# A one-core decoder block whose instruction order is planned: a stored order table, one wide constant table, other early buffers and loads

## The chip, the core and the metric

The kernel runs on one core of one Trainium2 chip. The metric is the device time of one execution in microseconds (us); the kernel before takes 552.94 us (median of three runs, 551.5 to 555.01). Five engines work side by side, each through its own instructions in their given order: TensorE (PE: matmuls, and the weight loads ahead of them, PEld), VectorE (DVE), ScalarE (ACT), GpSimd (POOL) and SyncE (SP), which here issues all DMAs. Engines wait for each other and for DMAs by semaphores.

## The reference

One decoder block on 256 tokens of width 1024, all in float32. Cut to what matters:

```python
h = rmsnorm(x, g_pre_mix)
z = h @ w_in                                  # 8248 columns, split into the branches' inputs
o_cmp, p_cmp = nsa_compressed(q, k0, v0, ...) # blocks of 32 tokens through a small MLP (w1, silu, w2)
o_slc = nsa_selected(q, k2, v2, ...)          # with 256 tokens all causal blocks are chosen
o_win = nsa_window(q, k4, v5)
y_nsa = gb[0] * o_cmp + gb[1] * o_slc + gb[2] * o_win
y_ml  = sigmoid(o_ml) * headnorm(mlstm(conv_silu(q, k), v, i, f)) * ml_head_g
kv    = rmsnorm(mem, g_mem) @ w_mem_kv        # the memory's keys (512 columns) and values (512)
y_mem = softmax(q_mem @ k.T * scale) @ v
y = gm[0] * (y_nsa @ w_proj_nsa) + gm[1] * (y_ml @ w_proj_ml) + gm[2] * (y_mem @ w_proj_mem)
x = x + rmsnorm(y @ w_out, g_post_mix)
h = rmsnorm(x, g_pre_ffn)
gate, up = split(h @ w_ffn_in)                # 2 x 2816 columns
x = x + rmsnorm((silu(gate) * up) @ w_ffn_down, g_post_ffn)
```

## The kernel before

**Products in three parts.** Every float32 operand of a product is split in two: `hi` is its copy rounded to the matmul's short float32 (ACT writes it: `whi` of a weight, `hh` of the normed x, `mh` of the memory), `lo` is what is left (DVE subtracts: `wlo`, `hl`, `ml`). A product is hi*hi + hi*lo + lo*hi, three matmuls into one PSUM tile (`mm3`). PSUM tiles of the dense products are called `pd` and `pss`; which of the two pools a tile takes says nothing of its content.

**Weights in units.** All weights stream from one array `W` in units of 128 x 1024 float32 (512 KB), one DMA each into a tile `raw` (four buffers), then `whi` (ACT) and `wlo` (DVE), four buffers each. `tmaj` multiplies tokens by four such units with the weights as the moving side (matmuls of 512 columns), `fpair` and `fcat` have the weights as the stationary side. The units' names are the matrices': `mem_k` 0 to 3, `mem_v` 0 to 3, `kv` 0 to 11 and so on.

**The stages.** (1) The memory: `memt` (the memory, transposed) is scaled to `mh`/`ml` by `mem_in`, which needs the gains in `vc` (from `vec`). The first three units of `mem_k` and their slices of `memt` come in halves, so that work can start early. The keys are 96 matmuls into two `pd` tiles, the values 48 matmuls of 512 columns into two `pss` tiles. The memory's sum of squares goes over `msq` (ACT squares, DVE adds), `col` (PE, two small matmuls by a column of ones), `rv` (DVE), `rm` (POOL, power -0.5) to `rbc` (PE, copies the row to all partitions). (2) The norm of x the same way: `sq`, `col`, `rv`, `rr`, `rbc`; then `xt` is scaled and split to `hh`/`hl`, eight slices of each. (3) `kv` 0 to 3, whose results go to `st` (ACT and DVE) and through `ph`, the small MLP of the compressed blocks, with weights `w1`. (4) Gates, memory attention, the three NSA attentions (four groups, two halves of 128 tokens each) with the mLSTM and the merge gates filled in between. (5) The three projections and the merge (`mrg`, `yh`/`yl`). (6) `w_out`: four `tmaj` products; `scaled` takes each result's sum of squares (`sq`, `ss`), its product with the gains (`zg`, `z`), and for 128 tokens at a time (`tb` 0 and 1) adds x into `xg`, transposes it (`ptx1`: four PE transposes for each half of the columns) and splits it to `xc` (hi and lo), the input of the FFN. (7) The FFN: `ffn_gate` and `ffn_up` for the first 512 columns, then 36 units by `fcat`, then `ffn_down`. Four units of the first `ffn_gate` product are kept in tiles `wq`.

**What sets the order.** `block_kernel` does not issue instructions as it is written. `Plan.record` notes each as an `Op` with its dependencies; `Plan.schedule` then lists them: at each step the engine that is free first takes, of its ops that are ready by a table of costs, the one of the lowest rank. A rank is the op's place in the code, moved by `plan.later(n)` (n places later) and by `boost` (a number for each op, which brings it forward). A tag's buffers are handed out in that order too. `Plan.replay` goes through an order with the same costs and finds what each PE op lost by waiting. `choose` tries 12 pairs of two cost settings (`matmul`, `slack`), takes the best by `replay`, and makes 40 rounds of random boosts along the chains that PE waited for, keeping those that `replay` finds no longer. `issue` emits the order that is left. All instructions are therefore issued in one line of the source (L511), and the rows of the profile are told apart by tile names.

**Where the change touches it.** `cs` (the constant table `cst` up to `K_M0`, with the identity `ident` in its first 128 columns), `rw` (the head gains and gate biases, a row that a DMA copies to all partitions), `w2t` (the compressed blocks' second weights), `mraw` (the masks), the DMAs ahead of the first norm, the tags of the two `w1` tiles (`G`, three buffers, of which `memt`, `mh` and `ml` are the first users), the three gain rows `g1`, `gp`, `go`, and the loop that transposes after `w_out`.

## Time and profile before

| | |
|---|---|
| three runs | 552.94, 551.5, 555.01 us |
| the profiled execution | 552.94 us, its span 551.1 us (first to last instruction) |
| PE busy | 539.2 us of the span (98%), 3164 matmul records |
| DVE, ACT, POOL busy | 422.5 (77%), 342.7 (62%), 20.5 us (4%) |
| DMA | 95.45 MB, mean 173 GB/s |
| granted TensorE clock, mean | 0.994 |

A matmul's row begins when its columns start to stream and ends, by a model, when the last result is out; rows of neighbours overlap. The step from one start to the next is what a matmul costs PE. A fp32 matmul that is not split in hi and lo (`ph`, `warm`) stands as two records. The profiled execution's own time is the median itself, so 552.94 us is what changes are counted from; 1.8 us of it lie around the span.

### The profile page before, as it was taken

How to read it: one execution, taken by the hardware profiler on the slowest of the kernel's cores; microseconds unless marked ns; L12 is line 12 of the kernel's file. 1: busy time of each engine (PE TensorE's matmuls, PEld its weight loads, DVE VectorE, ACT ScalarE, POOL GpSimd, SP SyncE). 2: the span in 40 equal slices, each digit the busy share in tenths (PEclk: the TensorE clock that was granted, in tenths of full speed). 3: DMA queues.
4: the chain of work that ended last, by engine and by line, in shares of the span. 5: the costliest groups of instructions: out<-in, count | busy, mean ns of one | idle time of the engine just before them, and what ended most of it. 6: DMA issues, size and time to landing. Idle time of an engine off the chain costs nothing.

```text
span 551.1 us, 8728 instructions
## 1 busy us (share of the span) xinstructions
PE 539.2 (98%) x3164; PEld 472.0 (86%) x3164; DVE 422.5 (77%) x813; ACT 342.7 (62%) x672; POOL 20.5 (4%) x34
## 2 busy tenths in 40 slices
PE   8899999999999999999999999999999999999995
PEld 8789999998989889889888888778888888888884
DVE  4797697589899897996888687975778787854543
ACT  6755777574699776875896444764666666643430
POOL 0010000000000100100100000000000000000000
PEclk9899999999999999999999999999999999999998
DMA  7966336734633354255254656753555555565512
GB/s 264 312 261 230 118 113 185 233 120 132 213 111 118 119 189 152 80 170 210 88 182 160 217 196 196 235 180 121 175 189 184 191 185 186 189 192 191 191 72 76
DMA packets 29419, 95.45 MB, mean 173 GB/s; under 512 B 3392, under 2 KB 6720, under 8 KB 29120
## 3 DMA queue, kind: packets, MB, share of 16 engines
q1 hardware_dynamic: 29376, 94.89, 52.0%
q8 instruction: 25, 0.41, 0.3%
q14 instruction: 18, 0.15, 0.1%
HBM read 92.78 MB, written 1.05 MB: 170 GB/s over the span
## 4 chain that ended last, share of the span: by engine, by line
PE 92%; DVE 3%; DMA 2%; issue 1%; ACT 1%; SPq 0%; DVEq 0%; ACTq 0%
PE pd L511 49%; PE pss L511 29%; PE sc L511 3%; PE pvn L511 2%; PE ptn L511 2%; PE ph L511 2%; DMA memt<-in_memT 1%; DMA raw<-in_W 1%; DVE wlo L511 1%; PE pn L511 1%; DVE wq L511 1%; PE psm L511 1%; DVE z L511 1%; PE pvm L511 1%; PE pq L511 1%
## 5 line engine op out<-in xcount | busy, mean ns | idle before, releaser
L511 DVE TENSOR_TENSOR wlo<-raw,whi 128x1024 fp32r<-128x1024 f32 (+1 forms) x161 | 193.6, 1206 | 66.7 <-ACT whi L511 63.3
L511 ACT ACTIVATE whi<-raw 128x1024 fp32r<-128x1024 f32 (+1 forms) x161 | 167.6, 1044 | 101.6 <-PE pd L511 57.0
L511 PE MATMUL pd<-hh,whi 128*128 128x256 f32 x224 | 64.3, 287 | 0.0
L511 PE MATMUL pd<-hh,wlo 128*128 128x256 f32 x224 | 64.1, 286 | 0.0
L511 PE MATMUL pd<-hl,whi 128*128 128x256 f32 x224 | 63.7, 285 | 0.2 <-DVE hl L511 0.2
L511 PE MATMUL pd<-whi,hh 128*128 128x512 f32 x144 | 58.8, 409 | 0.0
L511 PE MATMUL pd<-wlo,hh 128*128 128x512 f32 x144 | 58.3, 405 | 0.0
L511 PE MATMUL pd<-whi,hl 128*128 128x512 f32 x144 | 56.8, 397 | 0.0
L511 PEld LDWEIGHTS pd<-hl,whi 128*128 128x128 f32 x224 | 42.8, 191 | 0.6 <-DVE hl L511 0.4
L511 PE MATMUL pss<-xc,whi 128*128 128x512 f32 x168 | 43.2, 392 | 0.0
L511 PEld LDWEIGHTS pd<-hh,whi 128*128 128x128 f32 x224 | 42.8, 191 | 0.4 <-ACT hh L511 0.2
L511 PEld LDWEIGHTS pd<-hh,wlo 128*128 128x128 f32 x224 | 42.8, 191 | 0.2
L511 PE MATMUL pss<-whi,u 128*128 128x512 f32 x132 | 42.4, 392 | 0.0
L511 PEld LDWEIGHTS pss<-xc,whi 128*128 128x128 f32 x168 | 30.7, 189 | 5.4
L511 PE MATMUL pd<-xc,whi 128*128 128x512 f32 x120 | 31.9, 394 | 0.0
L511 PEld LDWEIGHTS pd<-whi,hl 128*128 128x128 f32 x144 | 27.1, 188 | 4.8
L511 PEld LDWEIGHTS pd<-whi,hh 128*128 128x128 f32 x144 | 27.2, 189 | 4.3
L511 PEld LDWEIGHTS pd<-wlo,hh 128*128 128x128 f32 x144 | 27.3, 189 | 3.9
L511 PEld LDWEIGHTS pss<-whi,u 128*128 128x128 f32 x132 | 24.8, 188 | 5.5
L511 ACT ACTIVATE pp<-sc,mx 128x128 f32<-128x128 f32 (+1 forms) x64 | 26.9, 433 | 1.4 <-DVE mx L511 1.4
L511 PE MATMUL pss<-wlo,u 128*128 128x512 f32 x66 | 25.9, 392 | 0.0
L511 DVE TENSOR_REDUCE mx<-sc 128x1 f32<-128x16 f32 (+2 forms) x96 | 22.3, 288 | 4.0 <-PE sc L511 3.8
(324 smaller groups left out, 1115.4 us busy)
## 6 DMA issues: line engine op xcount, KB each, us to landing
raw<-in_W SPq DMA_DIRECT2D x159, 512.0 KB, 4.2
w<-in_w SPq DMA_DIRECT2D x2, 1024.0 KB, 6.6
raw<-in_W SPq DMA_DIRECT2D x6, 256.0 KB, 4.0
xt<-in_xT SPq DMA_DIRECT2D x2, 512.0 KB, 8.5
kk<-kk SPq DMA_DIRECT2D x8, 128.0 KB, 4.7
x<-in_xN SPq DMA_DIRECT2D x2, 512.0 KB, 3.8
out<-z SPq DMA_DIRECT2D x8, 128.0 KB, 2.0
memt<-in_memT SPq DMA_DIRECT2D x6, 128.0 KB, 3.9
```

Of the source, the lines that this page charges most:

```text
L511: op.ins_ = getattr(op.real, op.method)(*map(arg, op.a), **{k: arg(x) for k, x in op.kw.items()})
```

## The change

It puts these things in place of the ones before:

- the order's table: `MATMUL, SLACK = 8.0, 30.0` and `BOOST`, a stored number for each of 241 ops; `choose` lists the ops once with these, and tries nothing. Two costs of the table are others (a DMA's cost and its landing time).
- the constant table `cst` is 720 columns wider: `rw` and `w2t` are slices of `cs` now, loaded with the masks' neighbours by one DMA, and their own two DMAs are gone. The three gain rows are stored 128 times in DRAM and read as plain tiles.
- in the code's order x comes ahead of `mem_v`, and `mem_v` 2 and 3, `kv` 0 to 3 and `w1` come ahead of the norms; `w1` lies in the tags `C` and `V`, one buffer each, whose next users are the convolution's `cy` and the values `vs`.
- the transposes after `w_out` have another rank: for `tb` 0 they stand 100 places earlier, for `tb` 1 as written.

The diff, cut:

```diff
+BOOST = {
+    0: 4320, 2: 90, 14: 580, 15: 560, 18: 4410, 19: 850, 20: 340, 96: 270, 97: 830, 122: 20, 127: 40, 128: 110, 129:
...
+}
+MATMUL, SLACK = 8.0, 30.0
-K_ID, K_TRI, K_RV, K_BM, K_M0, K_C1, K_MT, K_END = 0, 128, 256, 257, 261, 533, 549, 677
+K_ID, K_TRI, K_RV, K_BM, K_RW, K_W2, K_M0 = 0, 128, 256, 257, 261, 781, 973
+K_C1, K_MT, K_END = K_M0 + 272, K_M0 + 288, K_M0 + 416
...
-            return math.prod(views[0].shape) * 4 / 330.0
+            return math.prod(views[0].shape) * 4 / 410.0 + 70
...
-    START, TABLE, ISSUE, LAND = 570.0, 1283.0, 460.0, 1700.0
+    START, TABLE, ISSUE, LAND = 570.0, 1283.0, 460.0, 2000.0
...
-        best = None
-        for matmul in self.MATMUL:
-            for slack in self.SLACK:
...
-        return self.schedule(matmul, slack, boost)
+        order = self.schedule(MATMUL, SLACK, BOOST)
+        self.chosen = self.replay(order), MATMUL, SLACK, BOOST
+        return order
...
-    rw = one.tile([P, 520], F32, name="rw")
+    rw = cs[:, K_RW:K_RW + 520]
+    w2t = cs[:, K_W2:K_W2 + 192]
-    w2t = one.tile([P, 192], F32, name="w2t")
...
+    for h in range(2):
+        dma(out=xt[:, 4 * h:4 * h + 4, :], in_=xT[:, 4 * h:4 * h + 4, :])
     fetch(("mem_v", 0))
     fetch(("mem_v", 1))
-    for h in range(2):
-        dma(out=xt[:, 4 * h:4 * h + 4, :], in_=xT[:, 4 * h:4 * h + 4, :])
     dma(out=cs[:, 0:P], in_=cst[:, 0:P])
+    for u in (2, 3):
+        fetch(("mem_v", u))
+    fetch(("kv", 0))
+    fetch(("kv", 1))
+    w1t = []
+    for j, tg in enumerate("CV"):
+        t = bigt(tg, 1, [P, 16, P], F32, f"w1_{j}")
+        w1t.append(t)
+        dma(out=t, in_=w1[j].rearrange("p (a n) -> p a n", a=16))
+    fetch(("kv", 2))
+    fetch(("kv", 3))
...
-    fetch(("kv", 0))
-    fetch(("kv", 1))
     dma(out=wgt, in_=wg)
     dma(out=cs[:, P:], in_=cst[:, P:K_M0])
     mraw = work.tile([P, K_END - K_M0], F32, tag="sq", bufs=3, name="mraw")
     dma(out=mraw, in_=cst[:, K_M0:])
-    dma(out=rw, in_=bass.AP(tensor=row.tensor, offset=row.offset, ap=[[0, P], [1, 520]]))
-    dma(out=w2t, in_=w2)
...
-    w1t = []
-    for j in range(2):
-        t = bigt("G", 3, [P, 16, P], F32, f"w1_{j}")
-        w1t.append(t)
-        dma(out=t, in_=w1[j].rearrange("p (a n) -> p a n", a=16))
...
-    for t, i in ((g1, 520), (gp[:, 0, :], 520 + 2 * D), (go, 520 + D)):
-        dma(out=t, in_=bass.AP(tensor=row.tensor, offset=row.offset + i, ap=[[0, P], [1, D]]))
+    for i, t in enumerate((g1, gp[:, 0, :], go)):
+        dma(out=t, in_=row[i])
...
-        for q in range(2):
+        with plan.later(tb * 100 - 100):
+            for q in range(2):
...
-    row = np.concatenate([a[n] for n in ("ml_head_g", "ml_gate_b", "g_post_mix", "g_post_ffn", "g_pre_ffn")], axis=1)
+    row = np.stack([np.broadcast_to(a[n], (P, D)) for n in ("g_post_mix", "g_pre_ffn", "g_post_ffn")])
...
+    cst[:, K_RW:K_RW + 512] = a["ml_head_g"]
+    cst[:, K_RW + 512:K_RW + 520] = a["ml_gate_b"]
+    cst[:, K_W2:K_M0] = np.concatenate([w2k, w2k, a["cmp_w2_v"][0]], axis=1)
```

What the order becomes, at three places. The numbers behind the names tell tiles apart; they differ between the two programs. All rows stand in L511 before and in L505 after.

**SP, the queue of DMAs, from the tenth row on.** Before: `raw_137` is `mem_k` 2, `raw_204` is `mem_k` 3, `raw_222`, `raw_237`, `raw_263` and `raw_285` are `mem_v`, `xt` is x, `memt` 128x512 is the memory's last quarter.

```order
L511 DMA raw_137<-in_W 128x512
L511 DMA memt_97<-in_memT 128x256
L511 DMA raw_137<-in_W 128x512
L511 DMA xt_169<-in_xT 128x1024
L511 DMA memt_97<-in_memT 128x512
L511 DMA raw_204<-in_W 128x1024
L511 DMA raw_222<-in_W 128x1024
L511 DMA raw_237<-in_W 128x1024
L511 DMA xt_169<-in_xT 128x1024
L511 DMA cs_257<-in_cst 128x128
L511 DMA raw_263<-in_W 128x1024
L511 DMA raw_285<-in_W 128x1024
```

After: `raw_155` is `mem_k` 2, `raw_168` is `mem_k` 3, `raw_241` to `raw_308` are `mem_v`.

```order
L505 DMA raw_155<-in_W 128x512
L505 DMA raw_168<-in_W 128x1024
L505 DMA memt_74<-in_memT 128x256
L505 DMA raw_155<-in_W 128x512
L505 DMA memt_74<-in_memT 128x512
L505 DMA xt_214<-in_xT 128x1024 x2
L505 DMA raw_241<-in_W 128x1024
L505 DMA raw_268<-in_W 128x1024
L505 DMA cs_284<-in_cst 128x128
L505 DMA raw_291<-in_W 128x1024
L505 DMA raw_308<-in_W 128x1024
```

`mem_k` 3 has moved ahead of the last `memt` slices, and both halves of x stand between these and `mem_v`. In the rows ahead of these, `vc` has moved from fourth to third, and the first row is a slice of `memt` where it was a half unit of weights.

**DVE and PE, from the last keys to the first values.** On DVE before, `wlo_243` is the lo part of `mem_k` 3, `wlo_254` and `wlo_277` of `mem_v` 0 and 1, `msq` is the memory's sum of squares, `sq` that of x:

```order
L511 SCALAR_TENSOR_TENSOR ml_119<-memt_97,vc_102,mh_116 128x256 x2
L511 TENSOR_TENSOR msq_162<-msq_162,msq_234 128x1024
L511 TENSOR_TENSOR wlo_243<-raw_204,whi_239 128x1024
L511 TENSOR_TENSOR msq_162<-msq_162 128x512
L511 TENSOR_TENSOR wlo_254<-raw_222,whi_249 128x1024
L511 TENSOR_TENSOR msq_162<-msq_162 128x256
L511 TENSOR_TENSOR wlo_277<-raw_237,whi_265 128x1024
```

After, where `wlo_195` is the second half of `mem_k` 2 and `wlo_297` is `mem_v` 0:

```order
L505 TENSOR_TENSOR wlo_195<-raw_155,whi_187 128x512
L505 SCALAR_TENSOR_TENSOR ml_112<-memt_74,vc_98,mh_110 128x256 x2
L505 TENSOR_TENSOR msq_162<-msq_162,msq_233 128x1024
L505 TENSOR_TENSOR sq_247<-sq_247,sq_254 128x512
L505 TENSOR_TENSOR msq_162<-msq_162 128x512
L505 TENSOR_TENSOR vml_261<-ones_72,vml_261 128x8x2
L505 TENSOR_TENSOR sq_247<-sq_247,sq_274 128x512
L505 TENSOR_TENSOR msq_162<-msq_162 128x256
L505 TENSOR_TENSOR sq_247<-sq_247,sq_279 128x512
L505 TENSOR_TENSOR sq_247<-sq_247 128x256
L505 TENSOR_SCALAR rv_295<-col_289 128x2
L505 TENSOR_TENSOR wlo_297<-raw_241,whi_287 128x1024
```

The whole of both sums now stands between the last `ml` and the first `wlo` of the values. PE at the same place, after, where `pd_119` are the keys, `col` the sums and `pss` the values:

```order
L505 MATMUL pd_119<-mh_110,wlo_216 128x256
L505 MATMUL col_289<-ones_72,msq_162 128x1 x2
L505 MATMUL col_299<-ones_72,sq_247 128x1 x2
L505 MATMUL pss_302<-whi_287,mh_110 128x512
L505 MATMUL pss_306<-whi_287,mh_110 128x512
L505 MATMUL pss_302<-wlo_297,mh_110 128x512
```

Before, the first values followed the last keys at once, and the `col` rows stood singly among the values' matmuls; now all four are ahead of them.

**PE, from `w_out` to the FFN.** `pd` is the last `w_out` product, `ptx1` the transposes, `wq` the four kept units of the first FFN product. Before:

```order
L511 MATMUL pd_4111<-wlo_4078,yh_3793 128x512
L511 MATMUL pd_4111<-whi_4065,yl_3813 128x512
L511 MATMUL ptx1_4160<-cs_257,xg_3912 128x128 x4
L511 MATMUL ptx1_4167<-cs_257,xg_3912 128x128 x4
L511 MATMUL pss_4177<-wq_4046,xc_4172 128x512 x6
L511 MATMUL pss_4177<-wq_4082,xc_4172 128x512 x6
```

After:

```order
L505 MATMUL ptx1_4143<-cs_284,xg_3908 128x128 x4
L505 MATMUL pd_4107<-whi_4065,yh_3789 128x512
L505 MATMUL ptx1_4150<-cs_284,xg_3908 128x128 x4
L505 MATMUL pd_4107<-wlo_4084,yh_3789 128x512
L505 MATMUL pd_4107<-whi_4065,yl_3809 128x512
L505 MATMUL pd_4107<-whi_4065,yh_3789 128x512
L505 MATMUL pd_4107<-wlo_4084,yh_3789 128x512
L505 MATMUL pd_4107<-whi_4065,yl_3809 128x512
L505 MATMUL pss_4170<-wq_4042,xc_4152 128x512 x6
```

The eight transposes of `tb` 0 have moved up: six of the product's last matmuls stand behind the first four, five behind the second four.

More of the change, by code (lines that the diff above doesn't have):

```diff
@@ L450, in replay @@
         return max(op.end for op in order)
-    MATMUL, SLACK, ROUNDS = (2.0, 6.0, 10.0, 13.3), (0.0, 60.0, 130.0), 40
     def choose(self):
@@ L461, in choose @@
                 d.users.append(op)
-        best = None
-        for matmul in self.MATMUL:
-            for slack in self.SLACK:
-                order = self.schedule(matmul, slack, {})
-                length = self.replay(order)
-                if best is None or length < best[0]:
-                    best = length, matmul, slack, {}
-        length, matmul, slack, boost = best
-        rng = random.Random(0)
-        stale = True
-        for _ in range(self.ROUNDS):
-            if stale:
-                order = self.schedule(matmul, slack, boost)
-                self.replay(order)
-                waits = [(op.lost, op) for op in order if op.eng == "PE" and op.lost > 90 and op.why]
-                chains = []
-                for lost, op in waits:
-                    chain, d = [], op.why
-                    while d is not None and len(chain) < 16:
-                        chain.append(d.i)
-                        d = d.why or max((x for x, strict in d.deps.items() if strict), key=lambda x: x.end,
-                                         default=None)
-                    chains.append(chain)
-                stale = False
-            if not waits:
-                break
-            chain = rng.choices(chains, [w[0] for w in waits])[0]
-            step = rng.choice((20, 50, 100, 200, 400))
-            new = dict(boost)
-            for i in chain[:rng.choice((1, 2, 4, 8, 16))]:
-                new[i] = new.get(i, 0) + step
-            trial = self.replay(self.schedule(matmul, slack, new))
-            if trial <= length:
-                length, boost, stale = trial, new, True
-        self.chosen = length, matmul, slack, boost
-        return self.schedule(matmul, slack, boost)
+        order = self.schedule(MATMUL, SLACK, BOOST)
+        self.chosen = self.replay(order), MATMUL, SLACK, BOOST
+        return order
     def issue(self):
@@ L514, in block_kernel @@
 @with_exitstack
-def block_kernel(ctx, tc, order, xN, xT, memT, cst, vec, row, wg, w1, w2, W, out):
+def block_kernel(ctx, tc, order, xN, xT, memT, cst, vec, row, wg, w1, W, out):
     plan = Plan(tc)
@@ L1256, in block_kernel @@
         rs_.append(r)
[L1257 to L1264 removed]
+        with plan.later(tb * 100 - 100):
+            for q in range(2):
+                c = slice(512 * q, 512 * q + 512)
+                DVE.scalar_tensor_tensor(xg[:, tb, c], zg[tb][:, c], r, xg[:, tb, c], op0=ALU.mult, op1=ALU.add)
+                pt = ps_t([P, 4, P], "ptx1")
+                for j in range(4):
+                    PE.transpose(pt[:, j, :], xg[:, tb, (4 * q + j) * P:(4 * q + j + 1) * P], ident)
+                t = slice(tb * P, (tb + 1) * P)
+                split(xh[:, 4 * q:4 * q + 4, t], xl[:, 4 * q:4 * q + 4, t], pt)
     wq = [bigt(tg, n, [P, 2, 1024], F32R, "wq") for tg, n in (("Y", 2), ("Y", 2), ("V", 1), ("E", 2))]
```

10 lines of the change are left out of this document (1 added, 9 removed), and 22 rows, old and new, of the table BOOST.

## The prediction

> **What bounds the kernel now.** First the busy times of the page, then the same by stretches of the span (columns: us, then busy us and count of PE, PEld, DVE, ACT, POOL, then granted clock, DMA share, GB/s).
>
> ```profile
> PE 539.2 (98%) x3164; PEld 472.0 (86%) x3164; DVE 422.5 (77%) x813; ACT 342.7 (62%) x672; POOL 20.5 (4%) x34
> ```
>
> ```profile
> 15.60:19.00 3.40, 1.63 (x11) 1.22 (x10) 2.99 (x4) 2.27 (x3) 0.00 (x0) 1.00 0.98 388
> 19.00:22.50 3.50, 3.50 (x19) 3.50 (x18) 3.28 (x6) 2.73 (x4) 0.00 (x0) 0.51 0.86 257
> 46.00:103.00 57.00, 57.00 (x429) 54.68 (x429) 41.31 (x86) 38.21 (x74) 1.30 (x1) 1.00 0.50 158
> 103.00:345.00 242.00, 242.00 (x1466) 210.88 (x1465) 205.96 (x464) 165.90 (x382) 12.39 (x12) 1.00 0.48 158
> 345.00:364.00 19.00, 18.15 (x87) 14.69 (x86) 19.00 (x28) 12.96 (x21) 1.10 (x2) 1.00 0.72 235
> 364.00:544.00 180.00, 180.00 (x930) 153.71 (x929) 119.27 (x170) 94.51 (x146) 1.24 (x2) 1.00 0.51 167
> ```
>
> PE sets the time. From 46 to 345 and from 364 to 544 it is covered without a hole, so an order can win little there; what it can win lies in the first 46 us, where PE first stood still (1.63 of 3.40 us) and then ran at half clock (0.51), and around 345 to 364, where DVE is busy for all 19.00 us and PE is not. The timeline of PE shows the steps of the first stretch (start, us, then what, and the idle time with its releaser):
>
> ```profile
> 6.73 0.51 PE L511 MATMUL pd<-mh,whi 128*128 128x256 f32 x2 [1.15 <-ACT mh L511]
> 15.64 0.28 PE L511 MATMUL pd<-mh,wlo 128*128 128x256 f32 x1
> 16.98 0.39 PE L511 MATMUL pd<-mh,whi 128*128 128x256 f32 x1 [1.06 <-ACT whi L511]
> 17.44 0.28 PE L511 MATMUL pd<-ml,whi 128*128 128x256 f32 x1
> 18.43 0.39 PE L511 MATMUL pd<-mh,wlo 128*128 128x256 f32 x1 [0.71 <-DVE wlo L511]
> 22.37 0.45 PE L511 MATMUL pss<-whi,mh 128*128 128x512 f32 x1
> 22.89 0.39 PE L511 MATMUL pss<-whi,ml 128*128 128x512 f32 x1
> 31.18 0.39 PE L511 MATMUL pss<-whi,mh 128*128 128x512 f32 x1
> 35.36 0.28 PE L511 MATMUL pd<-hh,whi 128*128 128x256 f32 x1
> 36.61 0.38 PE L511 MATMUL pd<-hh,whi 128*128 128x256 f32 x1
> 37.24 0.38 PE L511 MATMUL pd<-hl,whi 128*128 128x256 f32 x1 [0.24 <-DVE hl L511]
> 44.89 0.28 PE L511 MATMUL pd<-hl,whi 128*128 128x256 f32 x1
> 45.51 0.74 PE L511 MATMUL ph<-st,w 128*128 128x75 f32 x4 [0.34 <-issue]
> ```
>
> The keys begin at 6.73, the values at 22.37, `kv` at 35.36. From 31.18 to 35.36 eighteen matmuls of 512 columns pass, 0.232 us each. Four waits are to be seen beyond a step's 0.12: 1.2 us up to 16.98 and 0.9 up to 18.43 for `mem_k` 3, whose DMA stands behind x; 0.5 at 37.24 for `hl`; 0.5 at 45.51, where `ph` follows too closely on the `kv` products that it is made from.
>
> **The change, part by part.** *The start, up to `kv`.* The rows of ACT and DVE that the new order is put together from:
>
> ```profile
> 6.17 0.91 ACT L511 ACTIVATE mh<-memt,vc 128x256 fp32r<-128x256 f32 x2 [1.18 <-DMA vc<-in_vec]
> 14.12 0.91 ACT L511 ACTIVATE mh<-memt,vc 128x256 fp32r<-128x256 f32 x2 [1.91 <-DMA memt<-in_memT]
> 14.66 0.88 DVE L511 SCALAR_TENSOR_TENSOR ml<-memt,vc,mh 128x256 fp32r<-128x256 f32 x2 [1.72 <-ACT mh L511]
> 16.01 1.23 DVE L511 TENSOR_TENSOR msq<-msq 128x1024 f32<-128x1024 f32 x1 [0.46 <-ACT msq L511]
> 18.29 0.68 DVE L511 TENSOR_TENSOR msq<-msq 128x512 f32<-128x512 f32 x1
> 20.03 0.42 DVE L511 TENSOR_TENSOR msq<-msq 128x256 f32<-128x256 f32 x1
> 20.66 1.23 DVE L511 TENSOR_TENSOR wlo<-raw,whi 128x1024 fp32r<-128x1024 f32 x1 [0.22 <-ACT whi L511]
> 22.01 1.48 DVE L511 TENSOR_TENSOR sq<-sq 128x512 f32<-128x512 f32 x2
> 24.90 1.15 DVE L511 TENSOR_TENSOR sq<-sq 128x512 f32<-128x512 f32 x2
> 35.59 1.26 DVE L511 SCALAR_TENSOR_TENSOR xt<-xt,vc,rbc 128x256 f32<-128x256 f32 x3
> 36.76 1.43 DVE L511 TENSOR_TENSOR hl<-xt,hh 128x256 fp32r<-128x256 f32 x4
> ```
>
> The keys' work waited for `vc` at 6.17; one place earlier in the queue it lands sooner, by about the one transfer that it passes, and I take 0.5 to 1 us. The last quarter of `memt` landed at 14.1. Ahead of it there stood half of x and not `mem_k` 3, 512 KB both; so it lands at 14.1 again, but with `mem_k` 3 there before it. The second half of `mem_k` 2 now comes behind `mem_k` 3. By the rows, DVE then has the second `wlo` of `mem_k` 2 and both last `ml` (0.88) done at about 16.1, and PE, after some 1.8 us of waiting at that half unit, ends the keys at about 19.1 (24 matmuls of 0.12 behind the last `ml`), where before the values began at 22.37.
>
> That lead is not kept. On DVE, `msq` 1.23, 0.68 and 0.42, `sq` 1.48 and 1.15, and two rows of under 0.2 stand ahead of the first `wlo` of the values: 5.3 us, less 0.08 of overlap at each of eight seams, 4.7. So that `wlo` runs from 20.8 to 22.0, and PE, whose four `col` rows are ahead of the values too, stands nearly idle from 19.1 to 22.0. The third matmul of the values, the first that needs `wlo`, comes at 22.0 where it came at 22.89: 0.9 gained. From there 46 matmuls of 0.232 and two pairs of `rbc`, which I take at 0.3 each (before, two pairs of `col` and three groups of `rbc` stood here and cost 1.8) end at 33.3: `kv` begins 2.1 us earlier than 35.36. DVE must have the first `wlo` of `kv` by then: four `wlo` of 1.15, eight `xt` of 0.42, five `hl` of 0.36 and about 1.3 of smaller rows are 11.1 us, 33.1; just in time. The bounds of this term: nothing gained, if x really holds the values up (below), and 3.2, if the first matmul's 1 us is kept through.
>
> *`kv` and `ph`.* The wait for `hl` goes, since DVE is through with it by 34.2, and 38 instead of 26 matmuls stand between the first `kv` pair and `ph`, 1.4 us more cover for a wait of 0.5: 1.0 gained together, at least 0.5.
>
> *The wide table.* It takes two DMAs out and adds no byte of use, and nothing needs its new columns ahead of `ph`. It stands behind `w1` in the queue now. I cost it at nothing, hidden by the values and the first `kv` products; if it or `wgt` were late, the gates' product behind `ph` would wait. The gain rows come from 1.5 MB of DRAM in place of 12 KB, but go to 128 partitions as before, in a stretch where the DMA share is 0.72: nothing. The tags of `w1` let it land before the values end and not after: no row waited for it, so nothing.
>
> *`w_out`.* Here the next rows speak:
>
> ```profile
> 351.51 0.60 ACT L511 ACTIVATE sq<-pd 128x512 f32<-128x512 f32 x1 [1.42 <-PE pd L511]
> 353.91 1.41 DVE L511 SCALAR_TENSOR_TENSOR xg<-zg,ss,xg 128x512 f32<-128x512 f32 x2
> 356.76 1.03 PE L511 MATMUL ptx<-cs,xg 128*128 128x128 f32 x8
> 358.28 0.73 PE L511 MATMUL pss<-wq,xc 128*128 128x512 f32 x2 [0.49 <-ACT xc L511]
> 359.38 3.02 PE L511 MATMUL pss<-wq,xc 128*128 128x512 f32 x12 [0.36 <-DVE xc L511]
> ```
>
> `xg` was done at 355.3, but PE transposed it at 356.76, behind the whole second product; then nothing was left to do while `xc` was made. Eight transposes take 0.87, yet 1.52 pass to 358.28; two matmuls take 0.46, yet 1.10 pass: 1.3 us lost. After the change, 18 matmuls (4.1 us) separate the first product's end from the transposes; `sq`, started at 351.51, to the end of `xg` took 3.8, so `xg` is ready in time, barely. Then five matmuls and twelve of `wq` that need only the first half of `xc` cover the rest, and DVE takes `xc` ahead of the next units' `wlo`. I take the 1.3 as gained; if `xg` is 0.5 late, 0.8.
>
> *The middle, 46 to 345.* The table reorders it all.
>
> ```profile
> L511 PE MATMUL pd<-whi,hh 128*128 128x512 f32 x144 | 58.8, 409 | 0.0
> L511 PE MATMUL pd<-wlo,hh 128*128 128x512 f32 x144 | 58.3, 405 | 0.0
> L511 PE MATMUL pss<-whi,u 128*128 128x512 f32 x132 | 42.4, 392 | 0.0
> ```
>
> Matmuls of one shape are 409 and 405 ns in the middle and 392 in the FFN: 144 x 17 and 144 x 13 ns, 4.3 us, is all that their neighbours (transposes, masks, late operands) cost them. Most of that is a weight load behind a short matmul, which another order moves and does not remove. I take nothing, with 4.3 gained and the same lost as bounds.
>
> The sum, against the profiled execution's own 552.9 (the median too): 2.1 + 1.0 + 1.3 = 4.4; **548.5 us**.
>
> **The rivals.** *Half clock again.* At 15.6 to 19.0 PE worked 1.63 of 3.40 us, and the next 3.4 us ran at 0.51. The new wait, 19.1 to 22.0 with few matmuls in it, is as long. If it brings another such stretch, values that take 0.232 take 0.43 in it, half of 3.4 us is lost: 1.7, 550.2. The earlier wait, in the keys, can bring it too, but then costs nothing, as PE would only reach the idle stretch later. Against it: how that stretch falls in the clock's windows, which the profile doesn't show ahead. The Trainium skill, page "TensorE: Matmul & The Clock Gate", section "What's actually happening", says that the clock falls to half after at least one idle window of some 3.4 us. By that rule the new wait, shorter and with matmuls in it, costs no clock and the sum stays; the row of 15.60:19.00, a window half at work, says that less is enough here.
>
> *The middle gains.* If the stored numbers spare two thirds of the 4.3: 2.9 more, 545.6. For it: PEld is busy 210.88 of 242, so loads are near the bound. Against it: no row of PE waits there as it is.
>
> *The start gives nothing.* x's 1 MB delays the values' weights, and if their first unit lands 2 us later than the 19 or so that I reckon with, the 2.1 is gone: 550.6. That the new start does not do what it says would be this.
>
> *Slower.* DVE in the middle:
>
> ```profile
> 143.00:163.00 20.00, 20.00 (x129) 17.49 (x127) 19.95 (x51) 15.44 (x30) 0.11 (x1) 1.00 0.35 119
> ```
>
> Where it has 0.05 us to spare in 20, an order that calls for a `wlo` earlier than DVE comes to it lets PE wait a whole `wlo`, 1.2 us, at each unit. Four such waits undo the gain, and nine make the kernel slower by over 1%, 559. Against it: the units' places among DVE's rows look alike in both orders.
>
> **How the numbers follow.** Chances: forecast 0.42 (547.4 to 549.8), half clock 0.22, middle 0.20, no gain at the start 0.11, slower 0.05. The range, 545.0 to 552.5, takes in the first four with their bounds. Within 1% (5.5 us, about what a measurement of this kernel tells from no change) lie most of the first, the second and the fourth; faster by more are the third and a tail of the forecast: 0.25; slower by more 0.05.
>
> **What would show it.** The first `kv` matmul at about 33.3; an idle PE for 2 to 3 us before the values, ended by DVE's `wlo`; the granted clock 1.00 or 0.51 behind it; no wait at `ph`; the first `wq` matmul right behind the last `pd`; no PE hole from 46 to 345. A values' wait ended by a DMA, or PE idle in the middle, would prove me wrong.

## The result and the profile after

| | before | after |
|---|---|---|
| median | 552.96 us (10 runs, 551.27 to 555.01) | 549.23 us (10 runs, 548.23 to 549.91) |
| profiled execution, its span | 552.94, 551.1 | 549.74, 547.9 |

The ratio after to before is 0.9933, 95% interval 0.9917 to 0.9949: 3.7 us less, within 1%. The forecast was 548.5. The total was close, yet its parts were not: the largest term, 2.1 us at the start, did not come, and other stages gave what it did not.

The page's busy times of the changed kernel, and the stretches of its span that stand against those shown of before (columns: us, busy us and count of PE, PEld, DVE, ACT, POOL, then granted clock, DMA share, GB/s):

```profile
PE 538.3 (98%) x3164; PEld 471.9 (86%) x3164; DVE 421.7 (77%) x813; ACT 345.4 (63%) x674; POOL 21.4 (4%) x34
...
15.60:19.00 3.40, 3.04 (x24) 2.85 (x24) 3.19 (x6) 3.38 (x7) 0.00 (x0) 1.00 1.03 409
19.00:22.50 3.50, 2.68 (x22) 2.39 (x21) 3.46 (x9) 2.98 (x5) 0.32 (x1) 1.00 0.58 229
22.50:26.00 3.50, 3.50 (x10) 2.52 (x10) 2.07 (x4) 0.76 (x1) 2.49 (x2) 0.53 0.40 143
...
46.00:103.00 57.00, 56.62 (x423) 53.90 (x423) 40.46 (x86) 39.25 (x74) 1.29 (x1) 1.00 0.51 151
103.00:345.00 242.00, 242.00 (x1471) 211.85 (x1471) 206.29 (x465) 167.88 (x384) 11.79 (x12) 1.00 0.48 159
345.00:364.00 19.00, 19.00 (x94) 15.80 (x93) 18.86 (x28) 12.27 (x20) 1.10 (x2) 1.00 0.67 207
```

The keys now run where PE stood still before (3.04 of 3.40 at 15.6 to 19.0). The half clock (0.53) has not gone; it came 3.5 us later and lies on the values. Around 345 to 364 PE is busy throughout and does 94 matmuls where it did 87. In the 242 us of the middle it does 1471 instead of 1466. Which waits are left, PE's list of waits says (us in total, times, longest):

```profile
...
PE pd L505 <- ACT whi L505: 0.6, 1, 0.6
PE col L505 <- DVE sq L505: 0.5, 1, 0.5
PE pm L505 <- DVE nm L505: 0.4, 1, 0.4
PE col L505 <- DVE msq L505: 0.4, 1, 0.4
PE pd L505 <- DVE ml L505: 0.4, 1, 0.4
```

The waits of `wq` for `xc`, of `ph` and of `kv` for `hl`, which stood in that list before (0.5 and 0.4, 0.3, 0.2), are out of it. A new one, of the small matmul `pm` for DVE's `nm`, lies at 82.7 in the stretch of 46 to 103. The timeline of the changed kernel's PE at the ends of the stages:

```profile
20.38 0.28 PE L505 MATMUL pd<-mh,wlo 128*128 128x256 f32 x1
21.02 0.61 PE L505 MATMUL col<-ones,msq 128*128 128x1 f32 x4 [0.36 <-DVE msq L505]
22.08 0.61 PE L505 MATMUL col<-ones,sq 128*128 128x1 f32 x4 [0.46 <-DVE sq L505]
22.55 1.05 PE L505 MATMUL pss<-whi,mh 128*128 128x512 f32 x2
23.40 0.68 PE L505 MATMUL pss<-wlo,mh 128*128 128x512 f32 x1
...
36.10 0.28 PE L505 MATMUL pd<-hh,whi 128*128 128x256 f32 x1
...
46.41 1.86 PE L505 MATMUL ph<-st,w 128*128 128x75 f32 x13
...
112.07 0.41 PE L505 MATMUL sc<-kk,qs 128*128 128x272 f32 x2
...
310.38 0.49 PE L505 MATMUL pty<-cs,mrg 128*128 128x128 f32 x3
...
356.46 0.39 PE L505 MATMUL pd<-whi,yl 128*128 128x512 f32 x1
356.69 4.26 PE L505 MATMUL pss<-wq,xc 128*128 128x512 f32 x18
...
380.29 0.27 PE L505 MATMUL ptu<-cs,ut 128*128 128x128 f32 x1
...
541.24 0.39 PE L505 MATMUL pd<-whi,u 128*128 128x512 f32 x1
```

From such rows of each profiled execution comes the table that the rest is read by: `kv` is its first matmul, `sc` the first score matmul, `pty` the first transpose ahead of `w_out`, `ptu` the first transpose of the FFN's `ut`, the end is the last matmul's start.

| us | `kv` begins | `kv` to `sc` | `sc` to `pty` | `pty` to `ptu` | `ptu` to end | `kv` to end |
|---|---|---|---|---|---|---|
| before | 35.36 | 76.43 | 199.40 | 71.52 | 161.49 | 508.84 |
| after | 36.10 | 75.97 | 198.31 | 69.91 | 160.95 | 505.14 |

Behind `kv` the change is worth 3.70 us, as much as the 3.7 of the medians. The start gave nothing that shows.

### The profile page after: what moved, and what is told of

Read it like the earlier page. It is cut to its first block, busy times and chain, and to the rows that moved or that the text cites. A ratio compares the mean times of both kernels' runs of the same rounds, so it can differ in the third digit from the quotient of the medians.

```text
span 547.9 us, 8746 instructions
## 1 busy us (share of the span) xinstructions
PE 538.3 (98%) x3164; PEld 471.9 (86%) x3164; DVE 421.7 (77%) x813; ACT 345.4 (63%) x674; POOL 21.4 (4%) x34
## 4 chain that ended last, share of the span: by engine, by line
PE 94%; DMA 2%; DVE 2%; SPq 1%; ACT 1%; issue 0%; DVEq 0%; ACTq 0%
PE pd L505 50%; PE pss L505 30%; PE sc L505 3%; PE pvn L505 2%; DMA memt<-in_memT 2%; PE ptn L505 2%; PE ph L505 2%; PE pn L505 1%; PE ptx L505 1%; SPq L505 1%; PE pvm L505 1%; PE pq L505 0%; PE psm L505 0%; DVE z L505 0%; PE pgf L505 0%; DVE sq L505 0%
## 5 line engine op out<-in xcount | busy, mean ns | idle before, releaser
L505 DVE TENSOR_TENSOR wlo<-raw,whi 128x1024 fp32r<-128x1024 f32 (+1 forms) x161 | 192.9, 1203 | 64.3 <-ACT whi L505 60.8
L505 ACT ACTIVATE whi<-raw 128x1024 fp32r<-128x1024 f32 (+1 forms) x161 | 167.2, 1044 | 95.9 <-PE pd L505 53.4
L505 PE MATMUL pd<-hh,wlo 128*128 128x256 f32 x224 | 64.0, 286 | 0.0
L505 PE MATMUL pd<-hl,whi 128*128 128x256 f32 x224 | 63.9, 285 | 0.0
L505 PE MATMUL pd<-hh,whi 128*128 128x256 f32 x224 | 63.9, 285 | 0.0
L505 PE MATMUL pd<-whi,hh 128*128 128x512 f32 x144 | 58.1, 407 | 0.0
L505 PE MATMUL pd<-wlo,hh 128*128 128x512 f32 x144 | 58.1, 403 | 0.0
L505 PE MATMUL pd<-whi,hl 128*128 128x512 f32 x144 | 57.0, 398 | 0.0
L505 PE MATMUL pss<-xc,whi 128*128 128x512 f32 x168 | 43.2, 392 | 0.0
L505 PEld LDWEIGHTS pd<-hl,whi 128*128 128x128 f32 x224 | 42.8, 191 | 0.2
L505 PEld LDWEIGHTS pd<-hh,whi 128*128 128x128 f32 x224 | 42.9, 191 | 0.2
L505 PEld LDWEIGHTS pd<-hh,wlo 128*128 128x128 f32 x224 | 42.8, 191 | 0.0
L505 PE MATMUL pss<-whi,u 128*128 128x512 f32 x132 | 42.1, 390 | 0.0
L505 PEld LDWEIGHTS pss<-xc,whi 128*128 128x128 f32 x168 | 30.7, 189 | 5.4
L505 PE MATMUL pd<-xc,whi 128*128 128x512 f32 x120 | 31.7, 394 | 0.0
L505 PEld LDWEIGHTS pd<-whi,hl 128*128 128x128 f32 x144 | 27.1, 188 | 4.7
L505 PEld LDWEIGHTS pd<-whi,hh 128*128 128x128 f32 x144 | 27.2, 189 | 4.4
L505 PEld LDWEIGHTS pd<-wlo,hh 128*128 128x128 f32 x144 | 27.2, 189 | 3.9
L505 PEld LDWEIGHTS pss<-whi,u 128*128 128x128 f32 x132 | 24.8, 188 | 5.3
L505 ACT ACTIVATE pp<-sc,mx 128x128 f32<-128x128 f32 (+1 forms) x64 | 27.0, 431 | 0.4 <-DVE mx L505 0.3
L505 DVE TENSOR_REDUCE mx<-sc 128x1 f32<-128x16 f32 (+2 forms) x96 | 22.9, 289 | 5.5 <-PE sc L505 5.2
L505 PE MATMUL pss<-wlo,u 128*128 128x512 f32 x66 | 25.7, 390 | 0.0
```

The lines of the kernel that those rows point to most:

```text
L505: op.ins_ = getattr(op.real, op.method)(*map(arg, op.a), **{k: arg(x) for k, x in op.kw.items()})
```

## The experiments

Where an edit says `MOVES`, the scheduler's list was left as in the kernel at hand, and single rows were moved in it: `(rows, mark)` puts the planner's operations with these numbers behind operation `mark` on their engine, or ahead of it for a negative number. Nothing else differs there, and the buffers stay where they were. The kernels of each group shared a chip with runs of the kernel before.

| run | median, us | ratio to before, 95% interval | `kv` begins | `kv` to `sc` | `sc` to `pty` | `pty` to `ptu` | `ptu` to end |
|---|---|---|---|---|---|---|---|
| values first | 551.37 | 0.9983 [0.9971, 0.9996] | 35.33 | 79.55 | 198.29 | 69.91 | 160.94 |
| split first | 549.42 | 0.9941 [0.9926, 0.9956] | 34.16 | 77.37 | 198.29 | 69.91 | 160.95 |
| padded | 548.49 | 0.9921 [0.9907, 0.9936] | 35.23 | 75.99 | 198.31 | 69.91 | 160.95 |
| `w_out` lumped | 549.0 | 0.9938 [0.9919, 0.9957] | 35.30 | 75.99 | 198.31 | 70.72 | 160.94 |
| DVE filled | 547.83 | 0.992 [0.9896, 0.9944] | 34.14 | 75.98 | 198.32 | 69.91 | 160.95 |
| both | 547.73 | 0.9912 [0.9896, 0.9928] | 34.80 | 75.97 | 198.34 | 69.91 | 160.94 |
| no table | 550.57 | 0.9971 [0.9955, 0.9988] | 36.38 | 75.30 | 199.51 | 70.12 | 160.94 |
| narrow tables | 548.93 | 0.9942 [0.9921, 0.9963] | 36.18 | 75.97 | 198.34 | 69.91 | 160.95 |
| `ph` early | 549.41 (one run) | | 34.64 | 77.11 | 198.32 | 69.92 | 160.94 |
| filled, padded | 547.98 | 0.9922 [0.9905, 0.9939] | 34.94 | 76.00 | 198.29 | 69.91 | 160.94 |

Two things are seen in it at once. Where a stage's rows are not touched, it takes the same time to 0.05 us, whatever happened ahead of it: PE is covered from `ph` on, so each shift of the start goes through to the end undiminished, and a stage can be compared between single executions. (The 79.55 of values first holds a stretch of half clock, shown there.) The start can not: with the same rows in the same order, `kv` begins at 35.30, 36.18 and 34.64 in the lumped, narrow and `ph` early runs.

**Values first**

```diff
+MOVES = [
+    ((154, 155), 157),                           # SP: x behind mem_v 0 and 1
+    ((223, 237), 168),                           # ACT: whi of mem_v 0, 1 ahead of x's squares
+    ((224,), 169), ((170, 171, 174), 224), ((238,), 174), ((252,), 189),   # DVE: wlo ahead of x's sums
+    ((225, 231, 226, 227, 228), 153), ((172, 173), 228),                   # PE: values, then col
+    ((187, 188), 246), ((191, 192, 176, 177), 255),
+]
```

> The changed kernel with one piece of its order altered and nothing else: the two halves of x are fetched behind the first two units of the memory values instead of ahead of them, ACT and DVE split those two units ahead of x's squares and sums, and PE's sums over columns stand among the values instead of ahead of them. Theory A (in the changed kernel DVE's sums of x, put ahead of the values' first wlo, empty PE at 20.4 to 22.5, and the half clock that follows costs the rest): values begin within 0.3 us of the last key (20.4 to 20.7), granted clock stays at 1.0, the first kv matmul moves from 36.1 to 32.5 to 33.5, and the time falls by 2.0 to 3.0 us against the changed kernel (549.2), to about 546.7. Theory B (DVE's total work from 17.5 on sets when kv can run, whatever its order): values begin early but wait for wlo units and kv waits for hl; gain at most 1 us, about 548.3. Theory C (the half clock does not come from the emptiness ahead of the values): it comes again at about the same time, the gain is about 1 us.

The values began 2.5 us earlier, at 20.08, and the kernel became 2 to 3 us slower than the changed one. `kv` to `sc` took 79.55 instead of 75.97. Its lists of PE's waits and DVE's timeline:

```profile
PE pd L542 <- DVE wlo L542: 1.8, 1, 1.8
...
PE pss L542 <- DVE wlo L542: 0.8, 1, 0.8
...
21.78 0.16 DVE L542 TENSOR_SCALAR rv<-col 128x2 f32<-128x2 f32 x1 [1.57 <-PE col L542]
...
26.44 0.16 DVE L542 TENSOR_SCALAR rv<-col 128x2 f32<-128x2 f32 x1 [0.70 <-PE col L542]
...
29.12 0.87 DVE L542 SCALAR_TENSOR_TENSOR xt<-xt,vc,rbc 128x256 f32<-128x256 f32 x2 [1.23 <-PE rbc L542]
...
36.50:40.00 3.50, 2.47 (x17) 2.47 (x18) 3.50 (x6) 2.40 (x4) 1.07 (x2) 0.87 1.01 424
40.00:43.50 3.50, 3.50 (x22) 3.50 (x22) 3.50 (x5) 0.63 (x1) 0.00 (x0) 0.64 1.02 400
```

DVE now waits 1.57, 0.70 and 1.23 us for PE's sums, x's scaling begins at 29.12 instead of 26.72, and everything that DVE has to do for `kv` comes that much later: PE pays it back as waits for `wlo`, one of them of 1.8 in `kv`. In this execution the half clock followed that wait, at 39.10 to 42.52 (the clock of 0.87 and 0.64 above), and took 1.5 of the 3.58 us by which `kv` to `sc` is longer. The median doesn't hang on it, since 9 of the 12 runs have a mean clock of 0.996 or more. Theory A is out; B names the right engine, and put its price too low; and the half clock is not bound to the place ahead of the values. Part of the loss is the way the edit was made: DVE's waits for `col` came from where it put these rows.

**Split first**: the transfers stay in the changed kernel's order.

```diff
+MOVES = [
+    ((223,), 182), ((224,), 183),                # ACT, DVE: mem_v 0 ahead of the last sums
+    ((225, 231, 226, 227, 228), 153), ((172, 173), 228), ((187, 188), 232), ((191, 192, 176, 177), 241),   # PE
+]
```

> The changed kernel with its transfers in the same order, but on ACT and DVE the first values' split ahead of the last of x's and the memory's sums, and on PE the column sums behind the first value matmuls. The weights land at 19.4 as in the changed kernel, so whi ends at about 20.5 and wlo at 21.8 instead of 23.2. Theory A: values begin at 20.6 instead of 22.55; the granted clock may still fall; kv begins 1.0 to 2.0 us earlier than 36.1, time about 547.7. Theory B (the chain of x: sums, column sums, the power, rbc, is what sets kv): that chain ends 1.0 to 1.5 us later and kv begins where it did or later; time 549.2 to 550.

Values at 20.22 and `kv` at 34.16, 1.9 earlier, but the time is that of the changed kernel (0.9941 to 0.9933). One row of its PE says where the gain went:

```profile
34.27 0.28 PE L538 MATMUL pd<-hl,whi 128*128 128x256 f32 x1
35.69 0.39 PE L538 MATMUL pd<-hh,wlo 128*128 128x256 f32 x1 [1.14 <-DVE wlo L538]
```

`kv`'s third matmul needs `wlo`, and DVE has it no earlier than in the changed kernel. Both theories have a half: PE could be helped, and DVE stood right behind it. (The clock stayed full in all six runs; what that spares, this wait takes back.)

**Padded**

```diff
+WARM = {153: 3, 173: 3, 188: 2}
+                for _ in range(WARM.get(op.i, 0)):      # behind these rows of PE, the first warm matmul again
+                    getattr(pad.real, pad.method)(*map(arg, pad.a), **{k: arg(x) for k, x in pad.kw.items()})
```

> The changed kernel with eight more of the matmuls of ones that it starts with (0.21 us each), put on PE around the column sums ahead of the values: three, three and two. They compute nothing that is used. They are 1.7 us of PE, 0.8 us of it in PE's waits there. Theory A (the empty stretch of PE ahead of the values costs the half clock at 22.7 to 26.1, some 1.5 us): the clock stays at 1.0, rbc and xt come earlier, and the time falls by 0.5 to 1.5 us against the changed kernel, to about 548.2, although PE has 0.9 us more to do. Theory C (the half clock is not set off by that stretch): clock 0.5 again in 22.5 to 26, and the time rises by 0.3 to 0.9 us, to about 549.9.

The same stretch of the span as above:

```profile
22.50:26.00 3.50, 3.50 (x24) 3.12 (x23) 2.18 (x5) 0.84 (x1) 2.47 (x2) 1.00 0.53 157
```

The clock is 1.00, 24 matmuls pass where 10 did. The values begin 0.74 later and `kv` 0.87 earlier. 548.49 is where theory A put it, though the interval of its ratio overlaps with the changed kernel's (0.9917 to 0.9949). That the clock is a matter of the order, and not luck, is shown by all the runs together: the mean granted clock of each run's span against the span. In the profiles a mean up to 0.995 goes with a stretch of half clock in the first 45 us, and one from 0.996 with none; what lacks to 1.000 there lies behind the last matmuls.

| | runs at 0.993 to 0.995 | their spans | runs at 0.996 to 0.999 | their spans |
|---|---|---|---|---|
| before, runs of this group | 9 of 17 | 550.0 to 551.9 | 8 of 17 | 549.5 to 550.2 |
| after | 8 of 10 | 546.7 to 548.1 | 2 of 10 | 546.4, 546.5 |
| start as in after: lumped, narrow, `ph` early | 4 of 11 | 547.6 to 549.2 | 7 of 11 | 546.4 to 547.6 |
| padded; filled and padded | 0 of 12 | | 12 of 12 | 545.7 to 547.1 |
| split first; both (below) | 0 of 12 | | 12 of 12 | 545.6 to 548.4 |

The changed kernel's start thus had it in 12 of 21 runs, and none of the 12 with idle matmuls. But none of the 12 runs of split first and both had it either: these add nothing to PE and put the first values ahead of the column sums. So the idle matmuls are one way to keep the clock, and another order is one too. Half clock is a matter of the single execution, in both kernels, and costs an execution some 1.1 to 1.4 us (the means of the two columns: 551.3 to 549.9 before, 547.6 to 546.5 after). A profile of either kernel can show it or not.

**DVE filled; both**

```diff
+MOVES = [((265,), 251), ((252, 266), -193)]     # filled: mem_v 2, 3 split in DVE's wait for rbc
```

"Both" has the moves of "split first" with `((265,), 251), ((238,), 174), ((252, 266), 189)` instead.

> The changed kernel with only ACT's and DVE's order altered: the split of the last two memory value units (whi on ACT, wlo on DVE, 1.2 us each on DVE) stands ahead of x's scaling, in the 2.15 us at 24.57 to 26.72 in which DVE waits for rbc. PE, SP and POOL keep their order. Theory P (PE bounds the values: 48 matmuls in a row from 22.55, with the half clock in them; kv follows the last of them at once): kv begins where it did, the time stays within 0.4 us of the changed kernel, about 549.2. Theory D (DVE bounds from 26.7 to 36): kv begins 1 to 2 us earlier, time about 547.7.

> The order of the values-ahead run (the first values split ahead of the last sums, PE's column sums among the values) together with DVE filled: the wlo of the memory values' units 2, 3 and 4 stand ahead of x's scaling, in the waits of 0.97 and 1.23 us that DVE had there for the column sums and rbc. Theory PD (PE and DVE bound the start together, within a microsecond of each other, and only moving both brings it): values from 20.2, kv from 33.5 to 34.2 and no wait of 1.1 us for kv's wlo behind it, ph0 2 us earlier than the changed kernel's 46.4, time about 547.2. Rival L (the landings of kv's weights, or the raw buffers that let them go, bound kv): ph0 at 45.6 or later, time 548.6 or more.

DVE's timeline of "both" in the place of the idle 2.15 us, and the stretch of its span:

```profile
24.44 2.35 DVE L541 TENSOR_TENSOR wlo<-raw,whi 128x1024 fp32r<-128x1024 f32 x2
26.71 0.22 DVE L541 CAST identb<-cs 128x128 bf16<-128x128 f32 x1
27.02 0.87 DVE L541 SCALAR_TENSOR_TENSOR xt<-xt,vc,rbc 128x256 f32<-128x256 f32 x2
...
22.50:26.00 3.50, 3.48 (x20) 2.65 (x18) 3.46 (x7) 1.76 (x2) 2.61 (x2) 1.00 0.68 197
```

With PE's order and DVE's fill together the wait of 1.14 is gone (`kv` to `sc` 75.97), and the six runs' clocks are 0.996 and more: 547.73, 0.9912, the shortest median of all, though the intervals still overlap with the changed kernel's. It is 0.5 longer than the 547.2 expected; `kv` began at 34.80, as the first `wlo` of the values let PE wait 0.5 and `rr` 0.3. "Filled" alone was to gain nothing (theory P) or 1 to 2 us (D). Its profiled execution had no half clock and began `kv` at 34.14; the changed order's execution without it (`ph` early) at 34.64. But there the values had begun at 22.02 and here at 21.52: from the first matmul of the values to `kv` it is 12.62 in both. So the fill gained nothing, as theory P has it; the two executions differ in what came ahead. The ratio, 0.992, is 0.0013 below the changed kernel's in an interval 0.0048 wide, which does not speak against it (one of the four runs had a clock of 0.995).

**Filled and padded**, the two edits above together.

> The changed kernel with DVE's wait filled (the last two wlo of the memory values ahead of x's scaling) and with the eight idle matmuls of ones around the column sums, which compute nothing that is used. Theory H (half clock in the values is a matter of single executions of the changed kernel, costs them 1.5 us, and dense PE work ahead of the values keeps it away; PE bounds the start): granted clock of the whole span 0.997 or more in every run, times between 546.8 and 548.3, median about 547.5, lower than the changed kernel's 549.2 by 1 to 2 us. Rival I (DVE's fill and the padding gain the same thing): no better than the padded run alone, 548.5.

547.98 and 0.9922: the padded run's ratio again. From the first matmul of the values to `kv` it is 11.94 in both, so here too the fill adds nothing. What theory H says of the clock holds, but for clocks of 0.996 in two runs; its gain of both together does not come. On the time rival I is right.

**`w_out` lumped**

```diff
+MOVES = [((3293, 3294, 3295, 3296, 3297, 3298), -3305)]    # PE: last six matmuls ahead of the transposes
```

> The changed kernel with one move undone on PE: the last six matmuls of w_out's second half stand ahead of the eight transposes ptx1 of the first half, as in the kernel before; all other engines keep their order. Theory A (the six matmuls cover the copies of the transposes): PE is idle 0.8 to 1.0 us ahead of and behind the first wq matmul, the time rises by 0.9 to 1.6 us, to 550.1 to 550.8. Theory B (the copies were hidden anyway, the gain at w_out comes from elsewhere, the order of the other engines): within 0.3 us of 549.2.

```profile
355.00 1.03 PE L533 MATMUL ptx<-cs,xg 128*128 128x128 f32 x8
356.29 4.65 PE L533 MATMUL pss<-wq,xc 128*128 128x512 f32 x18 [0.25 <-ACT xc L533]
```

`pty` to `ptu` is 70.72 instead of 69.91: 0.81 of the stage's 1.61 undone. The median, 549.0, is lower than the changed kernel's; at 0.8 us the start's scatter decides between medians, and only the stage tells. Theory A, a little below its range. The other half then lies in what this edit left in place: the order of the other engines, and PE's behind the first `wq`. Two runs of the kernel before look for it from the other side.

**The kernel before with `w_out`'s order**, first the transposes of `tb` 0 and their copies:

```diff
+MOVES = [((3307, 3308, 3309, 3310), 3294), ((3314, 3315, 3316, 3317), 3295),   # PE: ptx1 of tb 0
+         ((3311,), 3400), ((3318,), 3415), ((3312,), 3350), ((3319,), 3401)]   # ACT, DVE: its xc
```

> The kernel before with one place altered: at w_out the eight transposes ptx1 of the first half stand among the last matmuls of the second half, as in the changed kernel, and their copies xc on ACT and DVE ahead of the splits and the square that they stood behind; nothing else differs. Theory A (that is all of the change's gain at w_out): the stretch from the first pty to the first ptu, 71.52 in the kernel before and 69.91 in the changed one, is 69.9 to 70.3; time 1.2 to 1.6 us less than the kernel before. Rival B (half of it comes from the later order of wq and w_ff's units): 70.5 to 71.0, 0.5 to 1.0 us.

`pty` to `ptu` was 71.67, no gain at all. The waits at `wq` were gone and a longer one stood 5 us on:

```profile
356.48 3.34 PE L539 MATMUL pss<-wq,xc 128*128 128x512 f32 x14
361.11 0.63 PE L539 MATMUL ptx<-cs,xg 128*128 128x128 f32 x4 [1.29 <-DVE xg L539]
```

Both theories fail. The second half's `xg` now was late: DVE had a `wlo` of 1.2 us ahead of it, and PE reached the transposes sooner. The changed kernel differs in just that, so the rest of its order was put in:

```diff
+         ((3416,), 3332), ((3331, 3338), 3431),                                # DVE: wlo behind xg, xc of tb 1
+         ((3326, 3327, 3328, 3329), 3368), ((3333, 3334, 3335, 3336), 3369),   # PE: ptx1 of tb 1
+         ((3402, 3403, 3404, 3405), 3376)]                                     # PE: four of w_ff among wq
```

> The kernel before with the whole order of w_out and wq as in the changed kernel: besides the transposes of the first half among the last matmuls of w_out, the second half's eight transposes stand four wq matmuls later, four of w_ff's matmuls stand among wq's, and on DVE one wlo stands behind the second half's xg and xc instead of ahead. The rest is the kernel before. Theory A (the wait of 1.29 us that the earlier run showed ahead of the second half's transposes was the wait at wq in a new place; with DVE's wlo behind xg it goes): pty to ptu 69.9 to 70.2 instead of 71.52, time 1.3 to 1.6 us less than the kernel before. Rival B (it moves once more): 71.0 or more.

```profile
359.05 4.26 PE L540 MATMUL pss<-wq,xc 128*128 128x512 f32 x18
363.15 0.60 PE L540 MATMUL ptx<-cs,xg 128*128 128x128 f32 x4
```

70.13, no wait left: 1.39 of the 1.61, within the expected. (This execution ran at a lower clock from 15.6 to 26, mean 0.990 over the span, with `kv` at 36.74, so its total says nothing.) The gain at `w_out` is the order of one place, on three engines. Its first part alone brought nothing, and the changed kernel without PE's first part kept 0.80; the last 0.22 was not found.

**`ph` early**

```diff
+MOVES = [((351, 352, ..., 366), -399)]          # PE: ph ahead of the last twelve kv matmuls
```

> The changed kernel with the first sixteen ph matmuls put twelve kv matmuls earlier on PE, where they stood in the kernel before; the other engines keep their order. Theory A (the twelve matmuls cover st's copies on ACT, DVE and POOL): a wait of 0.3 to 0.7 us at the first ph comes back and the stretch from the first kv matmul to the first sc (75.97 in the changed kernel) grows by as much. Rival B (st was ready anyway, the wait went for another reason): no wait, 75.97 within 0.1.

```profile
44.34 3.87 PE L533 MATMUL ph<-st,w 128*128 128x75 f32 x28 [0.91 <-DVE st L533]
```

The wait is back, for `st`, and `kv` to `sc` grows by 1.14 us. Theory A, with more at stake than it said (0.3 to 0.7).

**No table**: `BOOST = {}`.

> The changed kernel with its stored table of boosts emptied: the scheduler alone, with the same two settings, sets the order. Theory T (the table is worth in the changed kernel about what the search's 90 boosts were worth before, and a little more): slower than the changed kernel by 3 to 12 us, most of it as PE waits of 0.5 to 2 us at the start and ahead of attention, none at w_out, whose order comes from the code's rank. Rival N (the table hardly matters, the scheduler's rules do the work): within 1.5 us of 549.2.

550.57, 1.3 us slower than the changed kernel's median, by the ratios 2.1. The intervals do not overlap, so the table is worth something, but less than the 3 to 12 of theory T and hardly more than rival N allows. By stages: `sc` to `pty` 199.51, as in the kernel before, so the 1.09 us of the middle are the table's; `w_out` 70.12 and the end 160.94, not the table's. Against that `kv` to `sc` is 0.67 shorter without the table, and `kv` began at 36.38 at full clock, 1.7 later than in the `ph` early run; how much of this one execution's start is scatter was not tried.

**Narrow tables**

```diff
-    dma(out=cs[:, P:], in_=cst[:, P:K_M0])
+    dma(out=cs[:, P:], in_=cst[:, P:K_RW])      # rw and w2t are tiles of their own again
+    dma(out=rw, in_=cst[:, K_RW:K_W2])
+    dma(out=w2t, in_=cst[:, K_W2:K_M0])
...
```

The rest of the edit lets the scheduler still see one transfer and then puts the two others behind it, so that the order is the changed kernel's. The two tables take 520 and 192 columns, 712 together.

> The changed kernel with its wide constant table taken apart again: the gate row and the compression weights have tiles of their own and come by two DMAs behind the table's (three instead of one, the same bytes); the order on every engine is the changed kernel's. Theory Z (the wide table is worth nothing, as predicted): time within 0.4 us of 549.2, the stretch from ph0 to the last matmul 494.8 as in the changed kernel. Rival M (the 0.5 us that the changed kernel gained in its last 60 us, from the first matmul on u to the last, 60.51 to 59.97, come from where the tables stand in memory): that stretch is 60.5 again, time 0.5 us more.

Every stage as in the changed kernel, 0.9942 to 0.9933: theory Z. The wide table is worth nothing that can be seen.

## Why the prediction was right in sum and wrong in its largest term

- **The start, forecast 2.1 gained: none.** `kv` was to begin at 33.3. This is the step that failed. First, the last quarter of `memt` was put at 14.1 "again", since 512 KB stood ahead of it either way; it landed at 15.6. The queue of DMAs came to it later: it was issued at 8.40 where it had been at 7.43.

```profile
7.43 0.43 SPq L511 DMA_DIRECT2D memt<-in_memT  x1
...
8.40 0.62 SPq L505 DMA_DIRECT2D memt<-in_memT  x1
...
15.62 0.91 ACT L505 ACTIVATE mh<-memt,vc 128x256 fp32r<-128x256 f32 x2 [0.45 <-DMA memt<-in_memT]
17.51 1.23 DVE L505 TENSOR_TENSOR msq<-msq 128x1024 f32<-128x1024 f32 x1 [0.21 <-ACT msq L505]
22.02 1.22 DVE L505 TENSOR_TENSOR wlo<-raw,whi 128x1024 fp32r<-128x1024 f32 x1
26.72 0.87 DVE L505 SCALAR_TENSOR_TENSOR xt<-xt,vc,rbc 128x256 f32<-128x256 f32 x2 [2.15 <-PE rbc L505]
```

  DVE's sums then take 17.5 to 22.0, 4.5 us where 4.7 were reckoned, so the first `wlo` ended at 23.2 and not at 22.0, and the keys at 20.5 and not at 19.1. The profiled execution is the latest: in the nine profiles with the changed kernel's transfers this `mh` starts at 14.55 to 15.62 (issued at 8.02 to 8.92), in the three with the old ones at 14.12 to 14.37 (7.33 to 7.66). Why the queue comes to it later was not tried. DVE's 11.1 us up to the first `wlo` of `kv` also left out its wait for `rbc`, 2.15 here. Second, the rival of the half clock came true in the profiled execution, 1.5 us. Third, and this is most of the 2.1, the baseline was itself an execution with 3.5 us at 0.51, which the sum counted as the program's and let the new order remove. An execution of the old start without half clock (the first `w_out` run of the kernel before) began `kv` at 34.07, one of the changed start without it (the `ph` early run) at 34.64. Their rows of the last quarter's `mh`:

```profile
14.37 0.91 ACT L539 ACTIVATE mh<-memt,vc 128x256 fp32r<-128x256 f32 x2 [2.07 <-DMA memt<-in_memT]
...
15.09 0.91 ACT L533 ACTIVATE mh<-memt,vc 128x256 fp32r<-128x256 f32 x2 [0.23 <-DMA memt<-in_memT]
```

  | from this `mh` to `kv`, us | full clock | with 3.4 us of half clock |
  |---|---|---|
  | old start | 19.70 | 21.24 (before) |
  | changed start | 19.55 | 20.48, 20.75, 20.76 (after, lumped, narrow) |
  | padded; filled and padded | 19.84, 19.96 | |

  The forecast had 19.2 (14.1 to 33.3), so its working from the landing on was right to 0.35. But at full clock the new order gains only 0.15 over the old there, and the later landing takes more than that.
- **The half clock.** The trace shows it behind stretches with PE at 1.63 of 3.40 and 2.68 of 3.50 us, and not in the first `w_out` run of the kernel before, which has 1.07 in the same 3.40:

```profile
15.60:19.00 3.40, 1.07 (x6) 0.87 (x7) 2.94 (x4) 3.25 (x4) 0.00 (x0) 1.00 1.02 403
19.00:22.50 3.50, 3.50 (x26) 3.28 (x25) 3.50 (x7) 2.00 (x4) 0.00 (x0) 1.00 0.79 261
```

  These cuts are ours and not the clock's. In the six profiles that have it near the start, the half clock lasts 3.41 us (once twice that), and from one change of the clock to the next it is always a multiple of 3.41; where these steps fall differs between executions of one order (half clock from 22.53, 22.73 and 23.60 in lumped, after and narrow). Cut by these steps, the idle stretch of the kernel before is 15.64 to 19.06, just ahead of the half clock; in the first `w_out` run the steps are 13.44, 16.85 and 20.27, the wait is shared between two of them, and PE is busy for 2.14 and 2.34 us. Busy time alone does not sort the steps, as the rows' modelled ends fill short gaps. The widths of the matmuls that start in a step do so nearly. Five steps before `kv` have 2304 to 2824 columns, and half clock follows each. Of the seven with 3076 to 3328 at full clock, one is followed by it (in values first); of those with more, none. A step full of values has some 7,700 (3.41 us at 0.227 for 512). This is a count from the 14 profiles, over the first 40 us; no run set out to test it.

  The Trainium skill, page "TensorE: Matmul & The Clock Gate", section "What's actually happening", says of a kernel's start that the window in which activity is watched is free-running, so that the same kernel ramps up differently from run to run. The runs here show the same for a fall in the middle of a kernel, 12 of 21 with the changed kernel's start. Its "at least one idle window" does not fit a step in which PE shows 2.60 of 3.42 us busy (19.31 to 22.73, after), and here the measurement decides.
- **`hl` and `ph`, forecast 1.0: both waits gone, 0.46 left of it.** With the place of `ph` undone the wait came back and cost 1.14, more than the 0.5 that it was before. Yet `kv` to `sc` as a whole gained only 0.46, since the new wait at `pm` (0.53 beyond a step) and a matmul of 256 columns (0.12) that stood behind `sc` before are in it too.
- **`w_out`, forecast 1.3: 1.61.** The first `wq` matmul stands right behind the last `pd`, as listed. The reason given, cover by five matmuls and twelve of `wq` with DVE's `xc` ahead of `wlo`, was needed but not enough: the kernel before with just this gained nothing until the second half's `xg` went ahead of a `wlo` too.
- **The wide table, gain rows, `w1`, forecast 0:** the table is 0 within what can be seen; the other two were not tried alone.
- **The middle, forecast 0 of 4.3: 1.09 gained**, by the table, 0.12 of it the matmul that moved ahead of `sc`. No hole of PE appeared from 46 to 345 but `pm`'s.
- **The last stage, not in the sum: 0.54 gained.** Neither the table, nor the wide table, nor `w_out`'s order has it; the cause is open. All of it lies on the 264 matmuls on `u`, 0.230 us a step before and 0.228 after: 122 steps of 0.228 or less before, 209 after, the others up to 0.241.

So 4.4 was forecast and 3.7 came, and the nearness is in good part luck: 2.1 at the start and 0.54 from `kv` to `sc` were missing, and 1.09 in the middle, 0.54 at the end and 0.3 at `w_out`, which the sum did not have, made up for most of it. The rivals "half clock again" and "the start gives nothing" hit the place, at 0.33 together. The first did so with its mechanism, the second in its result alone: no wait of the values was ended by a DMA, and DVE went from the last sum to their first `wlo` without a pause (the row at 22.02).
